# Attention P times V in plain 32-bit on the two column halves of the array, with P transposed and copied once

## The chip, the cores and the metric

The kernel runs on one core of a Trainium2 chip. A core has a matrix engine (PE, whose weight loads appear as PEld), three engines for elementwise work (DVE, ACT, POOL), and SP, which issues the DMAs. PE multiplies a stationary operand (loaded as weights) with a moving one and writes to PSUM; DVE and ACT bring results from PSUM to SBUF. The metric is the time of one execution on the device in microseconds.

## The reference

One layer of a token mixer with a feed-forward part: 1024 latent tokens and 256 context tokens of width 1024, everything in 32-bit floats. Eight attention heads of 64 share two key/value heads; beside them runs a bidirectional chunkwise mLSTM with four heads. What the change touches is the second product of the attention:

```python
p_loc = jnp.exp(s_loc - m)
p_ctx = jnp.exp(s_ctx - m)
inv = 1.0 / (p_loc.sum(-1, keepdims=True) + p_ctx.sum(-1, keepdims=True) + jnp.exp(sk - m))
o = (jnp.einsum('bnhgqk,bnkhd->bnqhgd', (p_loc * inv).astype(v.dtype), vw)
     + jnp.einsum('bnhgqc,bchd->bnqhgd', (p_ctx * inv).astype(v.dtype), vc))
...
mix_x = jnp.concatenate([att_x, ml_x], axis=-1) @ w_out[layer]
```

A query block of 128 tokens sees its own and the two neighbouring blocks of keys (one neighbour at the ends) and all context keys: three (or two) plus two key tiles of 128.

## The kernel before

The kernel has three stages: input projections and mLSTM state (to about 293 us of the profile), attention with the mLSTM output beside it (to about 480 us, the output projection begins in it), and the feed-forward part.

Large products run on operands of type `fp32r`, rounded below full 32-bit precision; each such matmul leaves one record in the trace. Where full precision is wanted, an operand is split: `split` (L62) lets ACT round it into a high part (L64) and DVE subtract that from the raw value for a low part (L65), and the product is built from two or three fp32r matmuls. A matmul on plain 32-bit operands needs no split.

The attention goes through 16 items, `items` (L714): row block `n` (eight of them), head group `g` (two). Loop pass `i` (L1052) does two things: the scores and softmax of item `i + 2` (class `Soft`: matmuls L972 and L973, masking on DVE L974, exponentials on ACT L983, normalisation on POOL L988), and the values of item `i` (class `Values`). The values come tile by tile of 128 keys, `nt` = 4 or 5 tiles an item, 76 in all:

- `tr(t)`: four transposes on PE (L1002) bring the tile of P for the four heads into a PSUM bank `pt` (three such banks, shared with the mLSTM values and the transposes of the mLSTM output), and `split` makes `th` on ACT and `tl` on DVE.
- `mm(t)`: two matmuls (L1012 with `th`, L1013 with `tl`) add to the bank `po`. Their stationary operand is `av2`, which holds V of the group's 64 columns twice, as high part and low part: 128 columns. So 64 rows of `po` hold the product with the high part of V, the other 64 that with the low part.
- `out()`: ACT copies one half of `po` (L1020), DVE adds the other (L1021) and writes the group's 64 rows of `mix`.

`av2` is made in the first stage by a split at L399. Beside that, passes 0 to 7 do the mLSTM output of a row block: scores (L862, DVE L867), values (L876, L880, then DVE L885 to L894 and ACT L892, L901), transposes back (L910, DVE L911). Passes 1 to 9 prepare slabs of the output weight: a load (L926) into the single buffer `wor`, a cast on ACT (L938), a subtraction on POOL (L939). The end of the loop and the last items carry the output projection (`omm`, rows `op`, L76 to L78).

The strings `PLAN_ML`, `PLAN` and `PLAN13` (L35 to L37) name the steps of a pass in the order in which they are handed over: T transposes, A scores, N softmax, M P times V, O its output, V mLSTM values, z, s, x other mLSTM steps, p the slab. From that a scheduler settles each engine's own order; an engine then works strictly through its own queue. What follows the loop stands in an order written out by hand (L1094 on).

Of the kernel before, what the change touches and what calls it, by code (L numbers as in the profile page):

```python
# [9 lines left out]
F32 = mybir.dt.float32  # L10
F32R = mybir.dt.float32r
# [3 lines left out]
ADD, SUB, MUL, MAX, MIN = ALU.add, ALU.subtract, ALU.mult, ALU.max, ALU.min  # L15

P = 128
# [3 lines left out]
NT = S // P  # L21
L = 256
NC_ = L // P
# [8 lines left out]
VSIL, VCONV, VGML, VBADA, VGPM, VGPF = 0, 16, 28, 32, 64, 72  # L32
VID = 80
NVEC = VID + P
PLAN_ML = "T0 A0 A1 A2 A3 T1 T2 T3 M0 M1 T4 V0 N0 M2 M3 M4 O z V1 w s N1 x p l"  # L35
PLAN = "T0 A0 A1 A2 A3 T1 T2 T3 N0 M0 T4 M1 M2 N1 M3 M4 O z p l"
PLAN13 = "T0 A0 A1 A2 A3 m T1 T2 P0 T3 N0 M0 T4 M1 P1 M2 N1 M3 P2 M4 O P3 l"  # L37
# [6 lines left out]
def body(tc, x, ctx, vecs, bcv, bada, gqm, gqf, wada, ws1, ws2, wt, wout, wfi, wfo,  # L44
         const, cosc, sinc, out):
    nc = tc.nc
    pe, act, dve, pool = nc.tensor, nc.scalar, nc.vector, nc.gpsimd
    dma = nc.sync.dma_start

    def open_pool(name, bufs=1, side="left", space=None):  # L50
        kw = dict(name=name, bufs=bufs, reuse_waits="tile")
        if space is not None:
            kw["space"] = space
        else:
            kw["side"] = side
        p = tc.tile_pool(**kw)
        return p, p.__enter__()
# [4 lines left out]
    def split(hi, lo, raw):  # L62

        act.copy(hi, raw)  # L64
        dve.tensor_tensor(lo, raw, hi.bitcast(F32), SUB)  # L65
# [77 lines left out]
    av2 = vp[1].tile([P, NT + NC_, 4, 64], F32R, name="av2")  # L143
    G = vp[1].tile([P, 4, 16, 4], F32, name="G")
    pool.memset(V[:, :, :, 128:129], 1.0)
    pool.memset(G, 0.0)
# [6 lines left out]
    hl = [htp[1].tile([P, 4, S], F32R, name=f"hl{i}") for i in range(2)]  # L153
# [48 lines left out]
    pts = {}  # L202
# [94 lines left out]
    for sec in (1, 0):  # L297
        pr = [pa.tile([4, 512], F32, name=f"pr{sec}{i}", tag="mm", bufs=4) for i in range(2)]
        for kt in range(KT):
            w = R(8 + kt, f"wa{sec}_{kt}", (D,))  # L300
# [16 lines left out]
            for n, (k, a, b) in enumerate(ops):  # L317
                if late and n < 2:
                    prep_t(1, True, (n,))
                for i in range(2):  # L320
                    r = pe.matmul(pr[i], a[:, k, :], b[:, i * 512:(i + 1) * 512], start=kt == 0 and n == 0,
                                  stop=kt == KT - 1 and n == len(ops) - 1)
# [19 lines left out]
        r = act.copy(r4[:, 0:512], pr[0])  # L342
# [7 lines left out]
        for q in range(2):  # L350
            t = (hcol, scol)[sec][:, q]
# [36 lines left out]
    def vrow(i):  # L388
        return V[:, i] if i < NT else Vc[:, i - NT]

    def s1(i):
        ps = slab(i, 272, w1h, w1l)
        sf = i + 2 if i < NT else i - NT
        sb = 9 - i if i < NT else 1 - (i - NT)
        dve.tensor_tensor(G[:, 0:2, sf, :], ps[:, 0:8].rearrange("p (k h) -> p k h", h=4),
                          bcr[:, 0:8].rearrange("p (k h) -> p k h", h=4), ADD)
        dve.tensor_tensor(G[:, 2:4, sb, :], ps[:, 8:16].rearrange("p (k h) -> p k h", h=4),
                          bcr[:, 8:16].rearrange("p (k h) -> p k h", h=4), ADD)
        split(av2[:, i, 0::3], av2[:, i, 1:3], ps[:, 16:144].rearrange("p (g v) -> p g v", v=64))  # L399
        act.copy(vrow(i)[:, 0, 0:128], ps[:, 144:272])  # L400

    NI = NT + NC_
# [19 lines left out]
    for i in range(NI):  # L422
# [7 lines left out]
        if i == 0:  # L430
            r = st[:, 13:14]
# [7 lines left out]
        if i in (1, 2):  # L439
            b = i - 1  # L440
# [138 lines left out]
    def T(i, name):  # L579
        return q2.tile([P, S], F32, name=name, tag=f"s{i}")  # L580
# [134 lines left out]
    NIT = len(items)  # L715
# [24 lines left out]
    for j, name in enumerate(TILES):  # L740
# [4 lines left out]
        ps = tproj(j, name in ("mk0", "mk1", "ak"))  # L745
        i = int(name[-1]) if name[-1].isdigit() else 0
# [4 lines left out]
        elif name == "ak":  # L751
# [14 lines left out]
        elif name.startswith("aq"):  # L766
            t = T(0, f"aq{i}")
# [6 lines left out]
        else:  # L774
            t = R(14 if i == 3 else 15, "so", (S,))
# [45 lines left out]
    for x_ in "hl":  # L821
        qa.tile([P, 4, P], F32R, name=f"t{x_}_", tag=f"pt{x_}", bufs=3)
# [4 lines left out]
    def bank():  # L827
        return pb.tile([P, 4, P], F32, name="pt", tag="pt", bufs=3)
# [161 lines left out]
    class Values:  # L990
        def __init__(self, i):
            self.n, self.g = items[i]
            self.pr = prs.pop(i)
            self.kb0, _, self.nb = blocks(self.n)
            self.nt = self.nb + 2
            self.po = pb.tile([P, 4, P], F32, name="po", tag="po", bufs=1)
            self.p = {}

        def tr(self, t):
            pt = bank()  # L1000
            for h in range(4):
                pe.transpose(pt[:, h, :], self.pr[:, h, 1 + t * P:1 + (t + 1) * P], ident)  # L1002
# [5 lines left out]
        def mm(self, t):  # L1008
            vt = self.kb0 + t if t < self.nb else NT + t - self.nb
            v2 = av2[:, vt, 2 * self.g:2 * self.g + 2].rearrange("p a v -> p (a v)")  # L1010
            th, tl = self.p.pop(t)
            pe.matmul(self.po, v2, th, start=t == 0, stop=False)  # L1012
            pe.matmul(self.po, v2, tl, start=False, stop=t == self.nt - 1)  # L1013

        def out(self):

            g = self.g
            rg, ot = slice(g * 64, g * 64 + 64), slice(64 - g * 64, P - g * 64)
            o2 = qa.tile([P, 4, P], F32, name="o2", tag="o2", bufs=1)
            act.copy(o2[rg], self.po[ot])  # L1020
# [20 lines left out]
    def omm(n, hf, ks):  # L1041

        h, l = mhl[n, hf]
        first, last = (0, 7) if n == 0 else (4, 3)
        for k in ks:
            j = 4 * hf + k
            for i in range(2):
                sl = slice(i * 512, (i + 1) * 512)
                mm3(ops_[n][:, sl], (h[:, k], l[:, k]), (wo[j][0][:, sl], wo[j][1][:, sl]), j == first, j == last)


    for i in range(NIT):  # L1052
        a = Soft(i + 2) if i + 2 < NIT else None
        b = Values(i)
        if i + 3 < NIT:
            q_load(i + 3)
        if i == NIT - 2:
            break
        wout_raw(i)
        for k in (PLAN_ML if i < NT else PLAN13 if i == NIT - 3 else PLAN).split():  # L1060
            op, n = k[0], int(k[1:] or 0)
            if op == "w" and i + 1 < NT:
                ml_load(i + 1)
            elif op == "T" and n < b.nt:
                b.tr(n)
            elif op == "M" and n < b.nt:
                b.mm(n)
            elif op == "O":
                b.out()
# [23 lines left out]

    order = tc.manual_schedule()  # L1094
    order.__enter__()
    def mm_t(b, *ts):
        for t in ts:
            b.mm(t)

    msplit(0, 1)  # L1100
    b.tr(0)
    b.tr(1)
    b.tr(2)
    omm(0, 1, range(1))
    mm_t(b, 0, 1)
    b.tr(3)
    omm(0, 1, range(1, 2))
    mm_t(b, 2, 3)
    b2 = Values(NIT - 1)
    b2.tr(0)  # L1110
    b.out()
    b2.tr(1)
    omm(0, 1, range(2, 3))
    b2.tr(2)
# [8 lines left out]
    b2.out()  # L1123
    order.__exit__(None, None, None)
    close(atp)
    close(aqp)
# [165 lines left out]
    th = {}  # L1292
# [73 lines left out]
    N1 = NT - 1  # L1366
# [359 lines left out]
    for p in range(4, HT):  # L1726
# [266 lines left out]
```

## Time and profile before

| | us |
|---|---|
| median of 3 runs | 1188.93 |
| lowest to highest | 1188.78 to 1191.32 |
| the profiled execution | 1189.32 |
| its span, first to last instruction | 1187.5 |
| granted PE clock over the span | 0.998 |
| PE busy in the span | 1164.6 |

A row of the profile's groups gives the line, the engine, the operation, what it writes and reads, shapes, count, then busy time, mean duration of one in ns, and the idle time before it with what ended it. A row of the timeline gives start and length in us. A count behind a row (x4) means neighbours that were joined. A matmul on plain 32-bit operands leaves two records, each with its weight load.

### The profile page before, as it was taken

To read this page: it belongs to the slowest core of one execution; us is meant where nothing else is said; L and a number is where in the kernel's file an instruction comes from. 1 tells how busy PE (TensorE), PEld (TensorE's weight loads), DVE (VectorE), ACT (ScalarE), POOL (GpSimd) and SP (SyncE) were. 2 spreads that over 40 slices of the span, in tenths; PEclk is the share of its full clock that TensorE was granted. 3 is DMA by queue.
4 is the path that set the end of the run, shared out by engine and by line. 5 is a ranking of instruction groups with operands and counts; after the bars stand their busy time and mean duration, and the time that the engine had idled before them with its cause. 6 is when DMAs were issued, how large, how long until landed. Compare 5 with 4: busy or idle time off the path is not lost.

```text
span 1187.5 us, 16397 instructions
## 1 busy us (share of the span) xinstructions
PE 1164.6 (98%) x5881; PEld 964.5 (81%) x5881; DVE 818.3 (69%) x1437; ACT 578.1 (49%) x1075; POOL 152.8 (13%) x204
## 2 busy tenths in 40 slices
PE   9899999999999989999999999999999999999997
PEld 3799888877888877888788888888888888888886
DVE  5864768863989984468767767776777656544566
ACT  6743442222877885777533334333333335434543
POOL 1550001225544550000000000000000000000000
PEclk9999999999999999999999999999999999999999
DMA  9522955648886713321242675656553557665853
GB/s 367 196 72 64 376 191 168 186 132 245 207 223 162 220 38 99 150 91 52 87 142 97 218 241 200 216 202 221 204 182 123 191 186 269 201 220 181 310 186 124
DMA packets 101992, 214.89 MB, mean 181 GB/s; under 512 B 10004, under 2 KB 39316, under 8 KB 100504
## 3 DMA queue, kind: packets, MB, share of 16 engines
q1 hardware_dynamic: 101912, 213.85, 54.4%
q8 instruction: 46, 0.75, 0.3%
q14 instruction: 34, 0.28, 0.1%
HBM read 157.19 MB, written 55.97 MB: 179 GB/s over the span
## 4 chain that ended last, share of the span: by engine, by line
PE 82%; DVE 10%; DMA 3%; ACT 2%; issue 2%; POOL 1%; SPq 0%; DVEq 0%; ACTq 0%; POOLq 0%
PE xv L78 8%; PE xv L76 8%; PE xv L77 8%; PE pt L78 6%; PE pt L76 6%; PE pt L77 6%; PE t L596 3%; PE t L595 2%; PE t L598 2%; PE op L78 2%; PE op L76 2%; PE op L77 2%; PE fx L76 2%; PE fx L78 2%; PE fx L77 2%
## 5 line engine op out<-in xcount | busy, mean ns | idle before, releaser
L65 DVE TENSOR_TENSOR fo<-fr,fo 128x1024 fp32r<-128x1024 f32 x77 | 92.7, 1222 | 70.9 <-ACT fo L64 70.6
L64 ACT CAST fo<-fr 128x1024 fp32r<-128x1024 f32 x77 | 79.7, 1052 | 73.9 <-PE pt L78 33.2
L595 PE MATMUL t<-hh,th 128*128 128x512 f32 x208 | 82.4, 396 | 0.0
L596 PE MATMUL t<-hl,th 128*128 128x512 f32 x208 | 81.7, 393 | 0.0
L1399 ACT CAST wS<-wr 128x512 fp32r<-128x512 f32 x88 | 54.2, 623 | 55.2 <-PE pt L78 36.6
L1401 DVE TENSOR_TENSOR wS<-wr,wS 128x512 fp32r<-128x512 f32 x88 | 60.4, 688 | 19.8 <-ACT wS L1399 19.7
L76 PE MATMUL xv<-tT,wS 128*128 128x512 f32 x168 | 65.6, 391 | 0.0
L78 PE MATMUL xv<-tT,wS 128*128 128x512 f32 x168 | 65.6, 391 | 0.0
L598 PE MATMUL t<-hh,tl 128*128 128x512 f32 x208 | 65.6, 393 | 0.0
L77 PE MATMUL xv<-tT,wS 128*128 128x512 f32 x168 | 65.5, 390 | 0.0
L76 PE MATMUL op<-woh,mh 128*128 128x512 f32 x128 | 51.0, 398 | 0.0
L77 PE MATMUL op<-wol,mh 128*128 128x512 f32 x128 | 50.0, 391 | 0.0
L78 PE MATMUL op<-woh,ml 128*128 128x512 f32 x128 | 50.0, 390 | 0.0
L1147 DVE TENSOR_TENSOR wr<-wr 128x512 f32<-128x512 f32 x66 | 45.5, 690 | 1.4
L1433 ACT ACTIVATE es<-es 128x512 f32<-128x512 f32 x22 | 13.9, 632 | 66.5 <-DVE es L1150 66.5
L595 PEld LDWEIGHTS t<-hh,th 128*128 128x128 f32 x208 | 39.1, 188 | 8.3 <-issue 0.3
L596 PEld LDWEIGHTS t<-hl,th 128*128 128x128 f32 x208 | 39.1, 188 | 7.8 <-issue 0.8
L598 PEld LDWEIGHTS t<-hh,tl 128*128 128x128 f32 x208 | 37.4, 188 | 6.9 <-issue 0.5
L76 PE MATMUL pt<-fo 128*128 128x512 f32 x110 | 42.8, 389 | 0.0
L77 PE MATMUL pt<-fo 128*128 128x512 f32 x110 | 42.8, 389 | 0.0
L78 PE MATMUL pt<-fo 128*128 128x512 f32 x110 | 42.8, 389 | 0.0
L972 PE MATMUL s<-k,qh 128*128 128x256 f32 (+1 forms) x128 | 40.5, 327 | 0.9 <-DVE sm L974 0.8
(1016 smaller groups left out, 3403.1 us busy)
## 6 DMA issues: line engine op xcount, KB each, us to landing
wr<-in_wfi SPq DMA_DIRECT2D x44, 512.0 KB, 4.8
wb<-in_wada SPq DMA_DIRECT2D x24, 512.0 KB, 5.8
s_d<-a SPq DMA_DIRECT2D x22, 512.0 KB, 6.8
bt<-in_wfo SPq DMA_DIRECT2D x44, 256.0 KB, 4.0
tb_d<-bt SPq DMA_DIRECT2D x11, 1024.0 KB, 3.9
fr<-s_d SPq DMA_DIRECT2D x44, 256.0 KB, 4.4
fr<-tb_d SPq DMA_DIRECT2D x44, 256.0 KB, 4.3
fr<-a_d SPq DMA_DIRECT2D x33, 256.0 KB, 4.5
```

Of the source, the lines that this page charges most:

```text
L64: act.copy(hi, raw)
L65: dve.tensor_tensor(lo, raw, hi.bitcast(F32), SUB)
L76: pe.matmul(ps, a[0], b[0], start=first, stop=False, **kw)
L77: pe.matmul(ps, a[0], b[1], start=False, stop=False, **kw)
L78: pe.matmul(ps, a[1], b[0], start=False, stop=last, **kw)
L595: pe.matmul(o, wh[:, kt], m[0], start=f, stop=False)
L596: pe.matmul(o, wh[:, kt], m[1], start=False, stop=False)
L598: pe.matmul(o, wl[:, kt], m[0], start=False, stop=l)
L972: pe.matmul(o, qh[:, h, :], k2[g][:, kc], start=True, stop=False)
L1147: dve.tensor_tensor(out, a, b, SUB)
L1399: act.copy(w[:, 0], raw)
L1401: dve.tensor_tensor(w[:, 1], raw, w[:, 0].bitcast(F32), SUB)
```

## The change

P is no longer split. `tr` copies the transposed tile once, ACT the even tiles and DVE the odd ones, into one of nine buffers `ts`. V is kept in plain 32-bit, 64 columns per group (`av`, half the size of `av2`), with one ACT copy in place of its split. P times V is one plain matmul per tile and group with 64 stationary columns: group 0 writes rows 0 to 63 of `po`, group 1 rows 64 to 127, and for each tile the two follow one another. It is done for both groups of a row block together, in the odd passes: `M0` does tiles 2, 1, 0, `M1` tiles 4, 3. One ACT copy takes the whole bank to `mix`. The step strings are new, with one for even and one for odd passes, and so is the order behind the loop.

```diff
-PLAN_ML = "T0 A0 A1 A2 A3 T1 T2 T3 M0 M1 T4 V0 N0 M2 M3 M4 O z V1 w s N1 x p l"
-PLAN = "T0 A0 A1 A2 A3 T1 T2 T3 N0 M0 T4 M1 M2 N1 M3 M4 O z p l"
+PLAN_ML = ("T0 A0 A1 A2 A3 T1 T2 T3 V0 N0 T4 z V1 w s N1 x p l", "T0 A0 A1 A2 A3 T1 T2 V0 N0 T3 M0 T4 z V1 w s M1 O N1 x p l")
+PLAN = ("T0 A0 A1 A2 A3 T1 T2 T3 N0 T4 N1 z p l", "T0 A0 A1 A2 A3 T1 T2 T3 N0 M0 T4 N1 M1 O z p l")
+NTS = 9
...
-        split(av2[:, i, 0::3], av2[:, i, 1:3], ps[:, 16:144].rearrange("p (g v) -> p g v", v=64))
+        act.copy(av[:, i], ps[:, 16:144].rearrange("p (g v) -> p g v", v=64))
...
-            th = qa.tile([P, 4, P], F32R, name="th_", tag="pth", bufs=3)
-            tl = qa.tile([P, 4, P], F32R, name="tl_", tag="ptl", bufs=3)
-            split(th, tl, pt)
-            self.p[t] = th, tl
+            self.p[t] = ts = qa.tile([P, 4, P], F32, name="ts_", tag="pts", bufs=NTS)
+            if t % 2:
+                dve.tensor_copy(ts, pt)
+            else:
+                act.copy(ts, pt)
...
-            pe.matmul(self.po, v2, th, start=t == 0, stop=False)
-            pe.matmul(self.po, v2, tl, start=False, stop=t == self.nt - 1)
...
-            act.copy(o2[rg], self.po[ot])
-            dve.tensor_tensor(mix[self.n][rg, 0:4, :], self.po[rg], o2[rg], ADD)
...
+        for t in ts:
+            vt = a.kb0 + t if t < a.nb else NT + t - a.nb
+            for g, x_ in ((1, b), (0, a)):
+                r = pe.matmul(pos[a.n][64 * g:64 * g + 64], av[:, vt, g], x_.p.pop(t), start=first and t == ts[0],
+                              stop=not more and t == ts[-1])
...
+    def pv_out(n):
+        act.copy(mix[n][:, 0:4, :], pos.pop(n))
...
-    mm_t(b2, 0, 1)
-    b2.tr(3)
+    pv(b, b2, range(4), False, False)
     omm(0, 1, range(3, 4))
-    mm_t(b2, 2, 3)
```

Two places show how the engines' queues change. The first is PE in pass 7, the second of the two passes of row block 3, from the transposes of its tiles on (`pr` is the pass's P, `th` and `tl` the split parts, `ts` the copies, `cs`, `qz`, `V`, `wl` the mLSTM values' operands). Before:

```order
L1002 MATMUL pt<-vec,pr__3728 128x128 x8
L1012 MATMUL po<-th__4111,av_91 128x512
L1002 MATMUL pt<-vec,pr__3728 128x128 x8
L1013 MATMUL po<-tl__4112,av_91 128x512
L1012 MATMUL po<-th__4144,av_91 128x512
L1013 MATMUL po<-tl__4145,av_91 128x512
L1002 MATMUL pt<-vec,pr__3728 128x128 x4
L1012 MATMUL po<-th__4153,av_91 128x512
L876 MATMUL pt<-cs_2558,qz_2970 128x129 x2
L880 MATMUL pt<-V,wl_4056 128x129 x2
L1013 MATMUL po<-tl__4154,av_91 128x512
L1012 MATMUL po<-th__4162,av_91 128x512
```

and now, in the same pass:

```order
L1001 MATMUL pt<-vec,pr__3627 128x128 x8
L876 MATMUL pt<-cs_2548,qz_2939 128x129 x2
L880 MATMUL pt<-V,wl_3919 128x129 x2
L1001 MATMUL pt<-vec,pr__3627 128x128 x4
L1019 MATMUL po<-ts__4011,av 64x512
L1019 MATMUL po<-ts__3852,av 64x512
L1019 MATMUL po<-ts__4004,av 64x512
L1019 MATMUL po<-ts__3845,av 64x512
L1019 MATMUL po<-ts__3973,av 64x512
L1019 MATMUL po<-ts__3814,av 64x512
L1001 MATMUL pt<-vec,pr__3627 128x128 x4
```

The P times V matmuls no longer stand singly between other work, but in a block of six, two for each tile, with the copies of passes 7 and 6 in turn; pass 6 has none.

The second is ACT about passes 8 and 9, around the casts of two slabs of the output weight (L938; L983 are the exponentials). Before:

```order
L938 CAST woh_4256<-wor_4104 128x1024
L983 ACTIVATE pr__4382,sm<-pr__4382,sm 128x641 x3
L64 CAST th__4399<-pt 128x512
L1020 COPY o_4361<-po 64x512
L64 CAST th__4432<-pt 128x512
L983 ACTIVATE pr__4382,sm<-pr__4382,sm 128x641
L64 CAST th__4441<-pt 128x512
L938 CAST woh_4370<-wor_4270 128x1024
L64 CAST th__4450<-pt 128x512
```

and now:

```order
L938 CAST woh_4107<-wor_3966 128x1024
L983 ACTIVATE pr__4111,sm<-pr__4111,sm 128x641
L1006 COPY ts__4165<-pt 128x512
L1006 COPY ts__4184<-pt 128x512
L1006 COPY ts__4225<-pt 128x512
L983 ACTIVATE pr__4209,sm<-pr__4209,sm 128x641 x3
L1006 COPY ts__4263<-pt 128x512
L938 CAST woh_4197<-wor_4120 128x1024
```

Copies of the even tiles take the place of the casts of all tiles, the copy of the output (L1020) is gone from the even pass, and a tile's copy still stands in the queue between the slab casts.

More of the change, by code (lines that the diff above doesn't have):

```diff
@@ L34 @@
 NVEC = VID + P
-PLAN_ML = "T0 A0 A1 A2 A3 T1 T2 T3 M0 M1 T4 V0 N0 M2 M3 M4 O z V1 w s N1 x p l"
-PLAN = "T0 A0 A1 A2 A3 T1 T2 T3 N0 M0 T4 M1 M2 N1 M3 M4 O z p l"
-PLAN13 = "T0 A0 A1 A2 A3 m T1 T2 P0 T3 N0 M0 T4 M1 P1 M2 N1 M3 P2 M4 O P3 l"
+PLAN_ML = ("T0 A0 A1 A2 A3 T1 T2 T3 V0 N0 T4 z V1 w s N1 x p l", "T0 A0 A1 A2 A3 T1 T2 V0 N0 T3 M0 T4 z V1 w s M1 O N1 x p l")
+PLAN = ("T0 A0 A1 A2 A3 T1 T2 T3 N0 T4 N1 z p l", "T0 A0 A1 A2 A3 T1 T2 T3 N0 M0 T4 N1 M1 O z p l")
+PLAN13 = "T0 A0 A1 A2 A3 m T1 T2 P0 T3 N0 M0 T4 P1 N1 P2 M1 O P3 l"
+NTS = 9
 WR = ((1, 2), (4, 5), (6, 7), (0, 3), (14, 15), (10, 13), (12, 8), (9, 11))
@@ L142, in body @@
     vp[1].tile([P, 88], F32, name="padv")
-    av2 = vp[1].tile([P, NT + NC_, 4, 64], F32R, name="av2")
+    av = vp[1].tile([P, NT + NC_, 2, 64], F32, name="av")
     G = vp[1].tile([P, 4, 16, 4], F32, name="G")
@@ L820, in body @@
     qa = atp[1]
-    for x_ in "hl":
-        qa.tile([P, 4, P], F32R, name=f"t{x_}_", tag=f"pt{x_}", bufs=3)
+    qa.tile([P, 4, P], F32, name="ts_", tag="pts", bufs=NTS)
     qa.tile([P, 80], F32, name="padq")
@@ L995, in __init__ @@
             self.nt = self.nb + 2
-            self.po = pb.tile([P, 4, P], F32, name="po", tag="po", bufs=1)
             self.p = {}
@@ L1002, in tr, with pv @@
                 pe.transpose(pt[:, h, :], self.pr[:, h, 1 + t * P:1 + (t + 1) * P], ident)
-            th = qa.tile([P, 4, P], F32R, name="th_", tag="pth", bufs=3)
-            tl = qa.tile([P, 4, P], F32R, name="tl_", tag="ptl", bufs=3)
-            split(th, tl, pt)
-            self.p[t] = th, tl
[L1008 to L1011, printed above, removed]
-            pe.matmul(self.po, v2, th, start=t == 0, stop=False)
[L1013 to L1020, printed above, removed]
-            dve.tensor_tensor(mix[self.n][rg, 0:4, :], self.po[rg], o2[rg], ADD)
+            self.p[t] = ts = qa.tile([P, 4, P], F32, name="ts_", tag="pts", bufs=NTS)
[3 more added lines that the diff above has]
+                act.copy(ts, pt)
+    pos = {}
+    def pv(a, b, ts, more, pin=True):
+        ts = [t for t in ts if t < a.nt][::-1]
+        first = a.n not in pos
+        if first:
+            pos[a.n] = pb.tile([P, 4, P], F32, name="po", tag="po", bufs=1)
+        for t in ts:
[3 more added lines that the diff above has]
+                              stop=not more and t == ts[-1])
+                if pin and (t != ts[0] or not g):
+                    tc.keep_in_program_order(r)
+    def pv_out(n):
+        act.copy(mix[n][:, 0:4, :], pos.pop(n))
     tc.keep_in_program_order(act.preload_act_table_set("natural_log_exp_and_others"))
@@ L1049, in omm @@
                 mm3(ops_[n][:, sl], (h[:, k], l[:, k]), (wo[j][0][:, sl], wo[j][1][:, sl]), j == first, j == last)
+    b = None
     for i in range(NIT):
         a = Soft(i + 2) if i + 2 < NIT else None
-        b = Values(i)
+        b0, b = b, Values(i)
         if i + 3 < NIT:
@@ L1059, in body @@
         wout_raw(i)
-        for k in (PLAN_ML if i < NT else PLAN13 if i == NIT - 3 else PLAN).split():
+        for k in (PLAN_ML[i % 2] if i < NT else PLAN13 if i == NIT - 3 else PLAN[i % 2]).split():
             op, n = k[0], int(k[1:] or 0)
@@ L1065, in body @@
                 b.tr(n)
[L1066 to L1069, printed above, removed]
+            elif op == "M" and i % 2:
+                pv(b0, b, ((0, 1, 2), (3, 4))[n], not n)
+            elif op == "O" and i % 2:
+                pv_out(b.n)
             elif op == "A" and a:
@@ L1095, in body @@
     order.__enter__()
-    def mm_t(b, *ts):
-        for t in ts:
-            b.mm(t)
     msplit(0, 1)
@@ L1104, in body @@
     omm(0, 1, range(1))
-    mm_t(b, 0, 1)
     b.tr(3)
-    omm(0, 1, range(1, 2))
-    mm_t(b, 2, 3)
     b2 = Values(NIT - 1)
     b2.tr(0)
-    b.out()
+    omm(0, 1, range(1, 2))
     b2.tr(1)
+    b2.tr(2)
     omm(0, 1, range(2, 3))
-    b2.tr(2)
+    b2.tr(3)
     msplit(1, 1)
     act.preload_act_table_set("sqrt_and_others")
-    mm_t(b2, 0, 1)
-    b2.tr(3)
+    pv(b, b2, range(4), False, False)
     omm(0, 1, range(3, 4))
-    mm_t(b2, 2, 3)
     ops_[1] = pb.tile([P, 1024], F32, name="op", tag="s", bufs=2)
     omm(1, 1, range(4))
-    b2.out()
+    pv_out(b.n)
     order.__exit__(None, None, None)
```

## The prediction

> **What bounds the kernel now.** I read the page's totals first, then the busy time by stage, then single stretches of the timeline. The totals:
>
> ```profile
> span 1187.5 us, 16397 instructions
> PE 1164.6 (98%) x5881; PEld 964.5 (81%) x5881; DVE 818.3 (69%) x1437; ACT 578.1 (49%) x1075; POOL 152.8 (13%) x204
> ```
>
> PE looks full, but a PE row lasts from its start to the end of its result, so rows overlap and a late start hides in the busy time. The change touches four stretches; for each: length, busy time (and count) of PE, weight loads, DVE, ACT, POOL, then granted clock, DMA share and GB/s.
>
> ```profile
> 299.00:410.80 111.80, 108.64 (x780) 96.17 (x780) 101.66 (x307) 91.61 (x257) 55.75 (x65) 1.00 0.78 202
> 410.80:444.70 33.90, 28.92 (x188) 24.66 (x187) 29.62 (x68) 28.64 (x62) 18.13 (x22) 1.00 0.27 73
> 444.70:480.00 35.30, 35.01 (x176) 28.37 (x175) 16.36 (x26) 18.58 (x34) 2.73 (x4) 1.00 0.40 140
> 480.00:1187.50 707.50, 701.41 (x3114) 578.71 (x3112) 472.22 (x656) 317.13 (x514) 0.96 (x1) 1.00 0.52 177
> ```
>
> The first row is the attention with the mLSTM work beside it (eight items and part of a ninth), the second attention alone (four items), the third its end with the output projection, the fourth the feed-forward part, which the change does not touch. In the first, DVE is busy 101.7 of 111.8 us (91%). I take one steady pair of items, a row block with its two head groups:
>
> ```profile
> 361.70:387.00 25.30, 24.93 (x182) 21.85 (x181) 22.92 (x71) 19.81 (x57) 10.91 (x14) 1.00 0.60 139
> ```
>
> How much of these 25.3 us does PE need? I take its pace from starts of neighbouring rows where nothing is late:
>
> ```profile
> 345.68 0.61 PE L876 MATMUL pt<-cs,qz 128*128 128x129 f32 x4
> 346.12 0.61 PE L880 MATMUL pt<-V,wl 128*128 128x129 f32 x4
> ...
> 347.04 0.34 PE L972 MATMUL s<-k,qh 128*128 128x384 f32 x1
> ...
> 347.62 0.34 PE L972 MATMUL s<-k,qh 128*128 128x384 f32 x1
> ...
> 349.88 0.71 PE L862 MATMUL s<-mq,mk 64*128 64x128 f32 x8
> ...
> 350.53 0.71 PE L876 MATMUL pt<-cs,qz 128*128 128x129 f32 x4
> ...
> 352.11 0.60 PE L1002 MATMUL pt<-vec,pr__3179 128*128 128x128 f32 x4
> ```
>
> ```profile
> L1002 PE MATMUL pt<-vec,pr__4596 128*128 128x128 f32 x20 | 3.2, 272 | 0.0
> ```
>
> Four mLSTM value records take 0.44 us, the scores of one head 0.58, the mLSTM scores 0.65. Four transposes last 0.60, a single one 0.272, so one follows another after (0.60 - 0.27) / 3 = 0.11. The fp32r matmul 128x512, and one in plain 32-bit, which leaves two records in the trace for each matmul written:
>
> ```profile
> 15.51 0.63 PE L321 MATMUL pr<-hh,cs 128*4 128x512 f32 x2
> 15.97 0.63 PE L321 MATMUL pr<-hl,cs 128*4 128x512 f32 x2
> ```
>
> ```profile
> 6.03 1.88 PE L321 MATMUL pr<-wa,cz 128*4 128x512 f32 x4
> ```
>
> ```profile
> L321 PE MATMUL pr<-wa,cz 128*4 128x512 f32 x24 | 11.3, 592 | 0.3 <-DMA wa<-in_wada 0.3
> ```
>
> Two fp32r matmuls take 15.97 - 15.51 = 0.46 us, so one takes 0.23. A plain record takes (1.88 - 0.59) / 3 = 0.43, a plain matmul 0.86. One item of five tiles thus needs 4 x 0.58 scores + 20 x 0.11 transposes + 10 x 0.23 P times V + 8 x 0.44 values + 0.65 + 0.44 (four more transposes) = 11.4 us, a pair 22.8. So PE loses **2.5 of 25.3 us to waiting**. What for shows in such places:
>
> ```profile
> 355.38 0.69 DVE L65 TENSOR_TENSOR tl__3600<-pt,th__3599 128x512 fp32r<-128x512 f32 x1 [0.58 <-ACT th__3599 L64]
> ...
> 356.13 0.19 PEld L1013 LDWEIGHTS po<-tl__3600,av 128*128 128x128 f32 x1 [0.54 <-DVE tl__3600 L65]
> ```
>
> ACT rounds a tile, then DVE subtracts, then PE may go on: the split is in the chain twice, and it is DVE's largest single load here.
>
> **The change, part by part.** *P is copied once.* Per tile an ACT copy and a DVE subtraction become one copy, on ACT for even tiles and DVE for odd ones. DVE's subtractions (L65) in the two attention stretches, and after them the additions (L1021) that merged the two halves of an output:
>
> ```profile
> 299.00:410.80 111.80, 29.26 (x44) 1.00 0.78 202
> 410.80:444.70 33.90, 15.30 (x23) 1.00 0.27 73
> ```
>
> ```profile
> 299.00:410.80 111.80, 5.48 (x8) 1.00 0.78 202
> 410.80:444.70 33.90, 2.76 (x4) 1.00 0.27 73
> ```
>
> What takes their place, by its nearest rows:
>
> ```profile
> L346 DVE COPY Vc<-pr 4x512 f32<-4x512 f32 x2 | 1.4, 675 | 0.1
> ```
>
> ```profile
> L1020 ACT COPY o<-po 64x512 f32<-64x512 f32 x16 | 9.3, 581 | 2.4 <-PE po L1013 2.1
> ```
>
> A DVE copy of 512 elements from PSUM takes 0.675, no less than the subtraction (29.26 / 44 = 0.67); an ACT copy 0.58. Per pair DVE loses ten subtractions and two additions and gains four copies: -10 x 0.67 - 2 x 0.69 + 4 x 0.675 = -5.4 us, from 22.9 to 17.5. ACT loses ten casts and two copies and gains six copies and one: -5 x 0.58 = -2.9, from 19.8 to 16.9. Neither can be the bound after that. The copies have nine buffers; the pair's tenth tile needs one that the P times V block ahead of it on PE has read, so this adds no wait.
>
> *P times V.* Per tile and pair of groups, four fp32r matmuls (0.92 us) become two plain ones of 64 columns. Alone these would take 2 x 0.86 = 1.72; side by side 0.86. The one place in this trace where matmuls of 64 columns alternate between the column halves, in plain 32-bit, is the state update, with its neighbours and its single duration:
>
> ```profile
> 206.41 0.39 PE L598 MATMUL t<-hh,tl 128*128 128x512 f32 x1
> 206.72 1.10 PE L704 MATMUL pu<-V,mkc 128*64 128x129 f32 x16
> 207.76 0.50 PE L598 MATMUL t<-hh,tl 128*128 128x512 f32 x1
> ```
>
> ```profile
> L704 PEld LDWEIGHTS pu<-V,mkc x112: 132/136/137, 206.7 to 286.1; 128*64 128x64 f32 x112
> L704 PE MATMUL pu<-V,mkc x112: 271/273/325, 206.7 to 286.2; 128*64 128x129 f32 x112
> ```
>
> Sixteen records take 1.10 - 0.27 = 0.83 us, 0.055 each, where the full-width L876 of the same 129 elements took 0.11 each: two run at once. The way in costs 206.72 - 206.41 - 0.23 = 0.08, the way out (207.76 against 207.55 + 0.11) 0.10. I take 0.86 per tile pair, and 0.18 per block, two to three blocks per pair of items: 5 x 0.86 + 2.5 x 0.18 = 4.75 against 20 x 0.23 = 4.60, so **+0.15 us per pair**. The bounds are 4.3 (no cost of changing) and 8.6 plus blocks (no overlap at 512 columns).
>
> On the hiding of weight loads the Trainium skill speaks against this: "TensorE: Matmul & The Clock Gate", Part 3, The mechanism, has a load overlap a running matmul only where the row groups differ, and the two halves share all rows. By that rule the loads would stand in the open. By that the sum would end at 1202 (below) instead of 1181. The trace disagrees: 16 loads of 0.136 are 2.2 us, and the whole block took 1.10.
>
> *What is late next.* PE's need per pair is 22.8 + 0.15 = 23.0, so at most 2.3 us of 25.3 go. P times V now sits in the odd item alone: without it PE needs 9.1 us in the even item, against DVE's 17.5 / 2 = 8.8 and ACT's 8.4, so there the three still hand work to one another nearly in step, and I leave 1.0 us of waiting per pair. Gain 1.3 to 1.4 per pair; the first stretch holds 111.8 / 25.3 = 4.4 pairs: **6 us** (bounds 0 and 10). DMA, busy 0.78 of that stretch, then comes to 0.82, and stays hidden.
>
> *Attention alone, 410.8 to 444.7.* Four items need 4 x (2.32 + 2.2 + 2.3) = 27.3 of 33.9 us. Most of the rest lies where ACT stands at the cast of a w_out slab, with the casts of P queued behind it:
>
> ```profile
> 407.63 2.40 POOL L939 TENSOR_TENSOR wol<-wor,woh 128x1024 fp32r<-128x1024 f32 x1
> ...
> 410.17 0.55 SPq L926 DMA_DIRECT2D wor<-in_wout  x1
> ...
> 415.56 1.04 ACT L938 CAST woh<-wor 128x1024 fp32r<-128x1024 f32 x1 [2.27 <-DMA wor<-in_wout]
> ...
> 416.68 2.40 POOL L939 TENSOR_TENSOR wol<-wor,woh 128x1024 fp32r<-128x1024 f32 x1 [1.87 <-ACT woh L938]
> ...
> 420.07 0.54 SPq L926 DMA_DIRECT2D wor<-in_wout  x1
> ...
> 424.78 1.04 ACT L938 CAST woh<-wor 128x1024 fp32r<-128x1024 f32 x1 [1.58 <-DMA wor<-in_wout]
> ```
>
> The slab has one buffer: POOL's subtraction ends (410.03), the load goes out, lands 5.4 us later, ACT 1.04, POOL 2.40, then the next. That ring is 9 us long whatever DVE does, and two items of 6.8 us of PE work run inside it in 20 us. I take **2 us** (bounds 0 and 3.5).
>
> *The rest.* In the first stage V's own split goes:
>
> ```profile
> L65 DVE TENSOR_TENSOR av<-slab,av 128x128 fp32r<-128x128 f32 x10 | 2.9, 285 | 2.4 <-ACT av L64 2.3
> ```
>
> That is 2.9 us of DVE beside a PE that is busy throughout; I take a tenth of it: 0.3. At the end PE had 35.01 of 35.3; there the last P times V starts with the tile transposed last and waits for its copy, 0.27 + 0.68, which takes the place of a wait for the last split: 0, bounds -1 and +1.
>
> The profiled execution took 1189.32 us, 0.4 above the median of 1188.93. Sum: 1189.3 - 6 - 2 - 0.3 = **1181 us**.
>
> **Rivals.** *Nearly all waiting goes:* 10 + 3.5 + 0.3 + 1 = 15 us, 1174. For it: DVE and ACT fall to some 70% of a pair; against it: the even item. *Hand-overs stay:* the three PSUM banks for transposes and mLSTM values, and the in-order queues, keep PE waiting as now although DVE idles; then about 2 to 3 us, 1187. For it: PE's wait now comes in pieces of half a microsecond behind single instructions. *Slower: the halves do not overlap at 512 columns.* Then a pair's P times V takes 8.6 + 0.45 instead of 4.6 us, 4.45 more. The first stretch needs 111.8 - 4.4 x 2.5 + 4.4 x 4.45 = 120.4, with some waiting 121 (+9); the second 27.3 + 8.9 = 36.2, with some waiting 37 (+3); the end, without slack and with some six and a half tile pairs, +6: 1207. It decides from the point where a quarter of the second matmul is left in the open (76 tiles / 2 x 0.86 = 33 us, of which 8.3 are the forecast's gain). Against it stands the L704 block; for it, that the block streamed 129 columns and not 512.
>
> *Weight loads in the open:* 152 records that each first wait 0.136 for their load are 21 us of PE work on top of the forecast, 1202. No row speaks for it, and L704 against it. It is what the Trainium skill's rule above would give.
>
> **How the numbers follow.** The forecast's own range, 1177 to 1185, gets 0.55; nearly all 0.13; hand-overs 0.20; no overlap 0.08; open loads 0.02; something not listed 0.02. The range runs from 1173 to 1188 and leaves the slower cases out. A measurement tells some 0.2%, 2.4 us: a third of the hand-over case lies within it. Faster 0.81, same 0.08, slower 0.11.
>
> **What would show it.** Right: plain 64-column rows in pairs a few ns apart, a block of six in about 2.6 us; DVE busy under 80 us where it was 101.7, PE's rows closer, a pair in 24 us; the w_out ring still 9 us. Wrong: 0.43 between single P times V rows; PE waiting for a bank with DVE idle; the feed-forward part longer than 707.5 us.

## The result and the profile after

| | before | after |
|---|---|---|
| median, us (4 runs each, side by side) | 1190.12 | 1181.13 |
| lowest to highest | 1188.78 to 1191.89 | 1181.01 to 1181.93 |
| ratio of the times, with its 95% interval | | 0.9926 [0.9913, 0.9938] |
| the profiled execution | 1189.32 | 1181.93 |

The change saves 0.74%, as much as was forecast. Its parts are another matter. The totals of the changed kernel's page:

```profile
span 1180.2 us, 16216 instructions
PE 1161.6 (98%) x5881; PEld 948.0 (80%) x5881; DVE 781.8 (66%) x1367; ACT 558.0 (47%) x1035; POOL 154.0 (13%) x204
```

In both kernels PE has 5881 records, a tile and group leaving two each time (before: one each with `th` and `tl`; now: the two records of a plain matmul). So a point in the work can be found by counting records: windows that begin at 0 and hold equally many PE records end at nearly the same PE work. That is a safer ruler here than a single event, since the change moves P times V past any of them; but records of different kinds differ in price, so which kinds have been done has to be counted too. Columns: length, then busy time (and count) of PE, weight loads, DVE, ACT, POOL, then granted clock, DMA share and GB/s. Before:

```profile
0.00:410.80 410.80, 399.30 (x2408) 332.74 (x2409) 300.06 (x690) 213.74 (x468) 130.97 (x177) 1.00 0.64 200
0.00:444.70 444.70, 428.22 (x2594) 357.40 (x2595) 329.68 (x756) 242.37 (x529) 149.10 (x199) 1.00 0.61 190
0.00:480.00 480.00, 463.23 (x2768) 385.77 (x2769) 346.04 (x782) 260.96 (x562) 151.83 (x203) 1.00 0.59 186
```

After:

```profile
0.00:300.10 300.10, 291.58 (x1630) 237.45 (x1631) 198.69 (x373) 122.14 (x211) 76.75 (x113) 0.99 0.59 198
0.00:408.40 408.40, 396.73 (x2408) 324.05 (x2409) 281.28 (x647) 202.87 (x445) 132.31 (x177) 1.00 0.64 201
0.00:436.04 436.04, 424.37 (x2594) 343.77 (x2596) 301.06 (x697) 226.49 (x496) 150.72 (x200) 1.00 0.62 194
0.00:472.40 472.40, 459.94 (x2768) 369.13 (x2769) 309.44 (x712) 240.25 (x522) 153.05 (x203) 1.00 0.60 190
```

At the 2408th record the changed kernel is 2.4 us ahead, at the 2594th 8.7, at the 2768th 7.6. At the last point the kinds done are the same in both. At the 2408th the changed kernel has done 10 P times V records fewer (76 against 86), one of the scores fewer and 11 transposes more; at the 2594th 5 P times V records and 3 of the output projection fewer and 8 transposes more. At 0.22 us for a record of P times V (0.43 a pair), 0.17 for the scores, 0.23 for the projection and 0.11 for a transpose, it still owes 1.1 and 0.9 us of work there, so at equal work it is some 1.3, 7.8 and 7.6 us ahead. The long stretch with the mLSTM work brought little, and the short one of attention alone 6.3 us by the count and 6.5 at equal work, the reverse of the forecast. A pair of items shows the same (182 PE records, first before, then after):

```profile
361.70:387.05 25.35, 24.98 (x182) 21.90 (x181) 22.97 (x71) 19.83 (x58) 10.96 (x14) 1.00 0.60 139
```

```profile
360.80:385.96 25.16, 24.39 (x182) 19.55 (x181) 18.32 (x63) 17.21 (x53) 11.04 (x13) 1.00 0.51 134
```

DVE has 4.65 us less to do, ACT 2.6, and the pair is 0.2 us shorter, where 1.3 to 1.4 was forecast. P times V itself looks as described, in a timeline of PE:

```profile
366.15 0.61 PE L880 MATMUL pt<-V,wl 128*128 128x129 f32 x4
366.69 0.64 PE L1019 MATMUL po<-ts__3681,av 128*64 128x512 f32 x1
366.70 0.64 PE L1019 MATMUL po<-ts__3526,av 128*64 128x512 f32 x1
367.17 0.59 PE L1019 MATMUL po<-ts__3681,av 128*64 128x512 f32 x1
367.18 0.59 PE L1019 MATMUL po<-ts__3526,av 128*64 128x512 f32 x1
367.70 0.66 PE L1001 MATMUL pt<-vec,pr__3299 128*128 128x128 f32 x4
```

The two groups' records start 10 ns apart: the halves overlap at 512 columns. The four L880 records are through at 366.15 + 0.44 = 366.59, the transposes start at 367.70: a block of one tile pair takes 1.11 us, 0.25 more than its 0.86.

In the second stretch, the slab loads, in timelines of SP and of ACT:

```profile
405.82 0.34 SPq L926 DMA_DIRECT2D wor<-in_wout  x1
...
412.89 0.34 SPq L926 DMA_DIRECT2D wor<-in_wout  x1
```

```profile
409.36 1.05 ACT L938 CAST woh<-wor 128x1024 fp32r<-128x1024 f32 x1 [0.38 <-DMA wor<-in_wout]
417.09 1.05 ACT L938 CAST woh<-wor 128x1024 fp32r<-128x1024 f32 x1
```

The ring is 412.89 - 405.82 = 7.1 us long, not 9 to 10, and ACT's waits of 2.27 and 1.58 us there are down to 0.38 and none. What PE waited for in that stretch, before (us in total, times, longest):

```profile
PE po L1012 <- ACT th__4450 L64: 2.1, 1, 2.1
PE po L1012 <- ACT th__4560 L64: 1.5, 1, 1.5
PE pt L1002 <- DVE tl__4645 L65: 0.6, 1, 0.6
PE pt L1002 <- DVE tl__4747 L65: 0.3, 1, 0.3
PE po L1012 <- DVE mix L1021: 0.3, 1, 0.3
```

That is 4.8 us; after, the same view of 408.4 to 436 has no row. SP's queue shows why the slabs came sooner. Before, three loads of queries stood ahead of one slab and two ahead of the next:

```profile
408.15 1.24 SPq L724 DMA_DIRECT2D qh<-aq_dh  x2
409.49 0.57 SPq L724 DMA_DIRECT2D ql<-aq_dl  x1
410.17 0.55 SPq L926 DMA_DIRECT2D wor<-in_wout  x1
```

In the changed kernel the scheduler puts both slabs ahead of these queries. The forecast had not read SP's order.

### The profile page after: what moved, and what is told of

Its sections match the earlier page's. It is cut to its first block, busy times and chain, and to the rows that moved or that the text cites. A ratio compares the mean times of both kernels' runs of the same rounds, so it can differ in the third digit from the quotient of the medians.

```text
span 1180.2 us, 16216 instructions
## 1 busy us (share of the span) xinstructions
PE 1161.6 (98%) x5881; PEld 948.0 (80%) x5881; DVE 781.8 (66%) x1367; ACT 558.0 (47%) x1035; POOL 154.0 (13%) x204
## 4 chain that ended last, share of the span: by engine, by line
PE 89%; DMA 4%; DVE 4%; ACT 1%; issue 1%; SPq 0%; POOL 0%; DVEq 0%; ACTq 0%
PE xv L79 8%; PE xv L77 8%; PE xv L78 8%; PE pt L77 6%; PE pt L78 6%; PE pt L79 6%; PE po L1019 3%; PE t L597 3%; PE t L596 3%; PE t L599 3%; PE pt L1001 3%; PE op L77 3%; PE op L79 2%; PE op L78 2%; PE fx L77 2%; PE slab L77 2%
```

## The experiments

Times are medians, ratios against the kernel before on the same chip. "At record n" is the time of that PE record in the profile, by windows like those above.

| run | us | ratio [95%] |
|---|---|---|
| halves in turn | 1190.07 | 0.9998 [0.9989, 1.0007] |
| one-tile blocks | 1188.39 | 0.9986 [0.9977, 0.9995] |
| free casts on DVE | 1198.70 | 1.0074 [1.0061, 1.0087] |
| additions on DVE | 1207.84 | 1.0145 [1.0131, 1.0158] |
| all copies on DVE | 1190.51 | 1.0000 [0.9991, 1.0009] |
| before, one copy | 1191.98 | 1.0009 [1.0000, 1.0019] |
| before, one copy in items 2 to 13 | 1182.13 | 0.9935 [0.9922, 0.9948] |
| the same and slab first | 1182.78 | 0.9937 [0.9924, 0.9950] |
| before, slab first | 1186.13 | 0.9959 [0.9946, 0.9971] |
| slab twice | 1182.67 | 0.9931 [0.9919, 0.9943] |
| last block later | 1180.69 | 0.9921 [0.9907, 0.9934] |
| whole blocks, last block later | 1180.25 | 0.9921 [0.9905, 0.9937] |

**Do the halves need to alternate in the queue?**

```diff
-        for t in ts:
-            for g, x_ in ((1, b), (0, a)):
+        for g, x_ in ((1, b), (0, a)):
+            for t in ts:
```

> Same work as the changed kernel (1181.1 us), but within a block of P times V all matmuls of one column half stand first in the queue, then all of the other; before, the halves alternated tile by tile. Theory A, only neighbours in the queue overlap: a block of k tile pairs then takes 4k-1 record times of 0.43 us instead of 2k; with 7 blocks of three pairs (2.15 us more each), 6 of two (1.29) and one of four (3.0) that is 25.8 us more work, 1200 to 1207 us. Theory B, each half works through a queue of its own that holds a whole block: records still in pairs a few ns apart, 1180 to 1182 us. In between, if only part of a block is looked ahead at.

Neither: 1190.07 us, 8.9 more than the changed kernel. The queue holds 4011, 4004, 3973 of group 1, then 3852, 3845, 3814 of group 0; PE's timeline:

```profile
395.11 1.07 PE L1019 MATMUL po<-ts__4011,av 128*64 128x512 f32 x2
396.02 0.59 PE L1019 MATMUL po<-ts__4004,av 128*64 128x512 f32 x1
396.03 0.64 PE L1019 MATMUL po<-ts__3852,av 128*64 128x512 f32 x1
...
396.88 0.59 PE L1019 MATMUL po<-ts__3973,av 128*64 128x512 f32 x1
396.94 0.59 PE L1019 MATMUL po<-ts__3845,av 128*64 128x512 f32 x1
...
397.80 1.02 PE L1019 MATMUL po<-ts__3814,av 128*64 128x512 f32 x2
```

The first matmul runs alone, then the fourth of the queue starts 10 ns behind the second and ahead of the third, and the last runs alone: four slots of 0.86 instead of three. Blocks of two tile pairs lost nothing. So PE starts a matmul of the free half past one that still waits for its own half, but no further; a lone slot in each of seven blocks (6.0 us), two in the last block of four (1.7) and one more in the first row block are 8.6 of the 8.9 us. It also prices the rival of halves that do not overlap: every slot that ran alone was paid in full.

**What does a block cost?** In one run the blocks are single tile pairs, each as soon as it can be (`M0` to `M4` spread over the pass):

```diff
-                pv(b0, b, ((0, 1, 2), (3, 4))[n], not n)
+                pv(b0, b, (n,), n < b.nt - 1)
```

> The changed kernel with P times V in blocks of one tile pair instead of three and two, each as soon as the tile of the odd item is copied: 12 to 14 more blocks on the way up to 437 us, as some blocks still meet in the queue. Price theory (a block costs 0.2 to 0.25 us beside its records, the way in and out between fp32 rows of the full array and column halves): 2.5 to 3.5 us more, 1183.5 to 1184.5 us. Cover theory (small blocks fall into places where PE waits for a bank): 1180 to 1182 us.

```profile
0.00:410.45 410.45, 400.83 (x2408) 323.67 (x2409) 282.64 (x648) 203.79 (x448) 133.25 (x178) 1.00 0.64 200
```

Up to there it has 19 blocks instead of 11 and is 410.45 - 408.40 = 2.05 us behind the changed kernel, which would be 0.256 a block. But it had reached record 1630, ahead of any block, 1.2 us sooner (298.9 against 300.1), and at record 2408 it has done four P times V records more and four transposes fewer, 0.4 us of work. From the same start and at equal work it is some 2.8 us longer, 0.35 a block, waits included. So blocks cost time, as the price theory has it, but this run alone does not fix the price. The other 5 us (by the medians) came later: seven more blocks, and a slab that came late again:

```profile
415.45 1.05 ACT L938 CAST woh<-wor 128x1024 fp32r<-128x1024 f32 x1 [5.13 <-DMA wor<-in_wout]
```

**What is the single copy worth alone?** The kernel before, with one copy and no other part of the change:

```diff
-            split(th, tl, pt)
-            self.p[t] = th, tl
+            if t % 2:
+                dve.tensor_copy(th, pt)
+            else:
+                act.copy(th, pt)
+            self.p[t] = th, th
```

> The kernel before the change with P rounded once by one copy (ACT even tiles, DVE odd) and its low part left out: both matmuls of a tile use the high part, so PE has the same work in the same places, but the subtraction on DVE and the second hand-over are gone. If the split in the chain is what cost the mLSTM stretch its 2 us: that stretch gains 2 or more, at equal PE work, and the whole comes to 1181 to 1186 us. If the pairs, blocks and new order brought it: 1187 to 1190 us.

The high part goes into both matmuls of a tile, so the result is about twice what it should be, and the run serves for the time alone. It came out at 1191.98 us, which says little, for in its profile PE lost 3.2 us in one wait at the start, where DVE's first maskings came late, and 4.4 in another behind the loop, where DVE stood before a late load of another tensor; and the granted clock was 0.50 for 3.4 us at 297.1 and again at 471.2:

```profile
PE s L971 <- DVE sm L973: 3.2, 1, 3.2
...
PE op L78 <- DVE ml L65: 4.4, 1, 4.4
```

Between record 1630 (302.3) and 2408 (408.6), clear of both places, it took 106.3 us, where the kernel before took 111.75. So the same with the single copy only in items 2 to 13:

```diff
+            one = 2 <= self.i < 14
-            split(th, tl, pt)
-            self.p[t] = th, tl
+            split(th, tl, pt) if not one else dve.tensor_copy(th, pt) if t % 2 else act.copy(th, pt)
+            self.p[t] = th, th if one else tl
```

> As the run with one copy in the kernel before (low part of P left out, both matmuls of a tile use the high part), but only for items 2 to 13, so that the engines' orders at the start and in the part behind the loop, where that run lost 3.7 and 6 us to other things, stay those of before. In SP's queue the last but one slab stands ahead of the queries of item 14, the last one behind those of item 15. If the split's hand-over and DVE's load are the larger cause: at equal PE work some 4 to 5 us less up to 425 us, the whole 1183 to 1187 us. If pairs and blocks are: within 1.5 us of before there.

```profile
0.00:405.55 405.55, 396.56 (x2408) 334.10 (x2409) 289.18 (x668) 209.34 (x454) 131.85 (x179) 1.00 0.64 202
0.00:436.30 436.30, 424.28 (x2594) 358.80 (x2595) 312.14 (x724) 234.11 (x508) 150.22 (x201) 1.00 0.62 194
```

```profile
359.95:383.54 23.59, 23.59 (x182) 21.76 (x181) 19.63 (x65) 18.58 (x54) 11.64 (x14) 1.00 0.65 161
```

1182.13 us, as fast as the whole change. It is 5.25 us ahead at record 2408, with the same work done but for one transpose and one score, where the changed kernel is 2.4 ahead by the count and 1.3 at equal work. ACT waits for no slab up to there in either kernel, so this much comes with the copy. The pair takes 23.59 us: 1.76 less than before and 1.57 less than with the changed P times V. What it wins after that record is not the copy's alone, since the last slab but one is issued ahead of the queries here too. And it drops P's low part and takes the high part twice. What the plain 32-bit product buys is that one copy holds all of P, and the column halves keep that product nearly as cheap as the split one.

**Load or hand-over?** All copies on DVE:

```diff
-            if t % 2:
-                dve.tensor_copy(ts, pt)
-            else:
-                act.copy(ts, pt)
+            dve.tensor_copy(ts, pt)
```

> The changed kernel with all copies of transposed tiles on DVE, none on ACT: DVE gets 40 more copies of 0.68 us, some 27 us over the attention, and goes to about 96 to 98 of 106 us in the first stretch; ACT loses as many of 0.58 us. Load theory: most of the gain in that stretch is lost, 1184 to 1187 us. Chain theory: a tile's chain is as long as before (0.68 instead of 0.58 for six of ten) and PE's remaining waits in the first stretch were for copies on ACT, so 1179.5 to 1182 us.

```profile
0.00:411.60 411.60, 398.36 (x2408) 324.18 (x2409) 292.83 (x671) 189.96 (x418) 132.66 (x178) 1.00 0.63 200
```

The whole gain is gone (1190.51). The chain theory as I had put it falls: a tile is still copied once, yet the kernel is 3.2 us later at record 2408 and loses most of the rest after it. But load by itself is not the answer either: up to that record DVE is busy 292.83 us here and 289.18 in the run with one copy in items 2 to 13, which is 6 us faster there. One difference is that there every second tile leaves its bank by the other engine; P times V differs too, and PE's order is not that of the changed kernel (15 blocks instead of 18), so this is not isolated. Two attempts to load DVE with work off the chain measured something else. The casts,

```diff
+            if t < 4:
+                dj = qa.tile([P, 4, P], mybir.dt.bfloat16, name="dj", tag="dj", bufs=1)
+                dve.tensor_copy(dj, mask[:, 0:4])
```

> The changed kernel with one more DVE instruction for each of the first four tiles of an item: a cast of 512 columns of the mask into a scratch tile that nobody reads, 64 in all, so that DVE has about as much to do as before the change, while no chain is longer. Load theory (the gain came because DVE was 91% busy): DVE in the first attention stretch goes from 78.6 us to about 95, and most of the 5.6 us won there come back, 1184 to 1187 us. Chain theory (the gain came because the split stood twice in the way between a transpose and its product): the stretch stays within 1.5 us of 106.2, 1181 to 1182.5 us.

were free to run early, and did (windows of that line alone: length, DVE busy and count):

```profile
300.00:363.70 63.70, 29.54 (x49) 0.94 0.66 180
363.70:480.00 116.30, 3.67 (x9) 1.00 0.49 144
```

so 49 of 64 stood in the first third, where DVE was busy 62.89 of 63.7 us and the kernel lost 15 us, and in the rest there was neither load nor loss. Not all of the 15 need be waiting: the granted clock was 0.94 there, which takes up to (1 - 0.94) x 63.7 = 3.8 us of PE's time. The additions, one for each of the first four tiles (`dve.tensor_tensor(dj, ts, mask[:, 0:4], ADD)`),

> The changed kernel with one more DVE instruction for each of the first four tiles of an item, an addition that reads the tile's copy and writes a scratch tile that nobody reads, 64 in all. Unlike the free casts of the run before, which went ahead in the queue, each must stay behind its copy, so DVE's load is spread as before the change (about 0.67 us each, 22.9 us per pair of items). Load theory: 1184 to 1188 us, PE waiting for DVE's masking and copies. Chain theory: 1181 to 1182.5 us.

stayed in place, but took 62.59 us in all instead of the planned 43, since some waited for POOL:

```profile
364.11 2.36 POOL L939 TENSOR_TENSOR woxl<-wor,woxh 128x1024 fp32r<-128x1024 f32 x1
364.49 2.53 DVE L1005 TENSOR_TENSOR dj<-ts__3536,mask 128x512 bf16<-128x512 f32 x1
```

Neither prices the load of before the change. In both PE paid for DVE work ahead of the maskings and copies (26.7 us for these 62.59), up to some 6 us of it by the granted clock, 0.97 over the 200 us from 290 to 490.

**The slab.** The kernel before, with only SP's queue changed:

```diff
+        with tc.issue_after(wlast[i - 3]) if i in (11, 12) else ExitStack():
+            if i + 3 < NIT:
+                q_load(i + 3)
```

> The kernel before the change (1190.1 us), with one edit: in SP's queue the loads of the queries of items 14 and 15 stand behind the loads of the last two slabs of the output weight, as the changed kernel has them, where before three and two of these query loads stood ahead. The queues of all other engines are the same, word for word. Queue theory (the changed kernel won 6.4 of its 8.6 us between 409 and 433 us because these two slabs were issued ahead of the queries, landed in 3.5 instead of 5.3 us, and ACT no longer stood at their casts with the copies of P behind it): 1184 to 1187 us, and ACT's two waits of 2.27 and 1.58 us shrink to under 1. Copy theory (won because half of the copies are on DVE and there are nine buffers): 1189 to 1190.5 us.

```profile
0.00:442.50 442.50, 427.95 (x2594) 358.13 (x2595) 329.96 (x757) 242.08 (x529) 148.75 (x199) 1.00 0.61 191
```

```profile
PE po L1012 <- ACT th__4450 L64: 1.1, 1, 1.1
```

1186.13 us, so 4.4 us (3.5 to 6.4 by the interval) from the order of five small loads; in the one profile it is 2.2 at record 2594, and PE's wait of 2.1 is 1.1, that of 1.5 is gone. The opposite, in the changed kernel, with both slabs loaded twice:

```diff
-                dma(wraw[j], wout[j])
+                [dma(wraw[j], wout[j]) for _ in range(1 + (i in (8, 9)))]
```

> The changed kernel (1181.1 us) with each of the last two slabs of the output weight loaded twice into the same buffer, the second load behind the first, so that ACT gets them some 3 us later; PE's order is the same up to about 418 us. Queue theory: ACT stands at the two casts again with copies of P behind it, PE loses 3 to 6 us there, 1184 to 1187 us. Copy theory: the copies on DVE and the buffers carry PE over it, 1181 to 1182.5 us.

```profile
414.31 1.05 ACT L938 CAST woh<-wor 128x1024 fp32r<-128x1024 f32 x1 [2.56 <-DMA wor<-in_wout]
426.99 1.04 ACT L938 CAST woh<-wor 128x1024 fp32r<-128x1024 f32 x1 [3.86 <-DMA wor<-in_wout]
```

```profile
PE po L1019 <- ACT ts__4467 L1006: 1.4, 1, 1.4
PE pt L1001 <- POOL pr__4479 L988: 0.5, 1, 0.5
```

ACT waits longer than it did before the change, and the waits that PE's view names are 1.9 us instead of 4.8; the kernel gives back 1.5 by the medians (1182.67), less than the intervals tell apart. In its profile, the slowest of its five executions (1183.88), it loses more: from record 2408 to 2594 it takes 31.0 us, 0.4 of it more work, against 27.6 in the changed kernel and 33.9 before. So a slab that comes later than before costs the changed kernel some 3 of the 6.5 us won in that stretch, and it keeps the rest: both theories held a part. Copy and slab order together, in the kernel before:

> The same with one more edit: in SP's queue the last slab too stands ahead of the queries of item 15, as in the changed kernel. So it has the single copy and the slab order of the changed kernel, but neither its column halves, nor its pairs and blocks, nor nine buffers. If copy and slab order make up the whole gain: 1181 to 1183 us. If the two overlap or the blocks carry a part of it: 1183.5 to 1186 us.

1182.78 us, not to be told from the run with the copy in items 2 to 13. The last slab was issued ahead of the queries and still came late (ACT waited 2.95 us for it; with the queries ahead 1.93), and so did the last but one, which stands ahead of its queries in both runs (3.03 against 1.18). In this profile the granted clock was also 0.50 for 3.4 us from 417.2 on, 1.7 us of PE's time. So the place in SP's queue is not all that sets when a slab lands; what else does stays open, and whether copy and slab order add up does too.

**The end.** In the changed kernel PE waits once behind the loop:

```profile
454.10 0.64 PE L1019 MATMUL po<-ts__4746,av 128*64 128x512 f32 x1 [0.78 <-DVE ts__4746 L1004]
```

```diff
-    pv(b, b2, range(4), False, False)
     omm(0, 1, range(3, 4))
+    pv(b, b2, range(4), False, False)
```

> The changed kernel with one edit at the end: the last block of P times V stands behind the eighth quarter of the first output projection instead of ahead of it. In the changed kernel PE stood there some 1.0 to 1.4 us for the copy of the tile that was transposed last. If that wait was real: 1179.7 to 1180.3 us and no wait at that block. If the work it is moved past hides nothing because the next product waits instead: 1181 us.

The wait is gone; 1180.69 against 1181.13 us is within the two intervals. The last run adds whole blocks: the transposes of the fourth tile pinned ahead of the first block in the mLSTM passes.

> The changed kernel (1181.1 us) with two edits: in the mLSTM passes the first block of P times V is no longer cut in two by the transposes of the fourth tile, which now stand ahead of it (16 blocks in all instead of 18), and the last block stands behind the eighth quarter of the output projection, as in the run that tried this alone (1180.7 us). SP's order of slabs and queries is that of the changed kernel. Price theory (a block costs about 0.25 us beside its records): 1179.7 to 1180.4 us. Rival: ahead of an unbroken block PE waits for the third tile's copies, which the cut had covered: 1181 us or more.

1180.25 us, the lowest median here, at 0.9921 [0.9905, 0.9937], but not to be told from the run before it, nor by the interval from the changed kernel (0.9926). In the profile, with two blocks instead of three in a pair, two passes take 24.82 us (from the first mLSTM score matmul, L862, of one pass at 350.61 to that of the next but one at 375.43) instead of 25.15 in the changed kernel (352.39 to 377.54): 0.33 for one block, waits included.

## Why the forecast came out, step by step

**The total** of 1181 was right by luck: two terms missed in opposite directions and nearly cancelled.

*P is copied once* was sized right: 1.3 to 1.4 us a pair forecast, 1.76 in the run that has only this, 5.25 us up to record 2408 against the term's 6. In the changed kernel, though, that stretch gained only 1.3 at equal work (2.4 from record 1630 on, which came 1.1 us late; 3.1 in the profile of the run with the last block later, the same code up to there), for the next two reasons. DVE's 17.5 and ACT's 16.9 us a pair came out at 18.3 and 17.2.

*P times V, +0.15 us per pair* was too small. The records run as read from L704, 0.43 a pair. But a block costs 0.25, not 0.18, and the scheduler cuts a pair's five tiles into three blocks, not two and a half: 3 x 0.25 + 5 x 0.86 = 5.05 against 4.60, +0.45.

*I leave 1.0 us of waiting per pair* failed by more. With 22.8 + 0.45 of work in 25.16 us, 1.9 are left, where the run with the single copy and the old P times V leaves 23.59 - 22.8 = 0.8. The view of PE's waits names 0.8 of the 1.9, the row below; the rest are gaps too small for it, and some may be work that 22.8 leaves out. The even item without P times V was seen as the weak place, and there it stands: PE wants a bank whose tile ACT has not yet copied.

```profile
383.07 0.30 PE L910 MATMUL pt<-vec,hs 128*128 128x128 f32 x1 [0.77 <-ACT ts__3891 L1006]
```

Together, 0.45 and 1.1, these give back 1.57 of the 1.76 us; that is near the rival "hand-overs stay", true in this stretch. That the waiting comes from the move of P times V into the odd pass was read from this row and the pair, not tried alone.

*Attention alone, 2 us*, measured 6.3 (6.5 at equal work), beyond its bound of 3.5. The step that failed is "that ring is 9 us long whatever DVE does": its length held 5.4 us for a load that stood behind queries in SP's queue, an order which the change moved. The slab order alone gave 2.2 in the profile and 4.4 by the medians. The run with one copy in items 2 to 13, which has one of the two slabs ahead, gave (444.7 - 410.8) - (436.3 - 405.55) = 3.15; the run with the copy and both slabs ahead, whose slabs came late and whose clock fell, 33.9 - (439.1 - 405.4) = 0.2. So the slabs have a large share in the 6.5; how the rest divides stays open.

*The end, 0 (bounds -1 and +1)*: (472.40 - 436.04) - (480 - 444.7) = +1.06 by the count, of which 0.9 is the work that the changed kernel still owed at record 2594; at equal work it is +0.2, with the wait of 0.78 above in it, so this term held. *V's split, 0.3*: not to be seen. Record 1630 comes 1.1 us later (300.1 against 299.0), with the same kinds done in both; but the run with one-tile blocks and the last run, with the same first stage, have it at 298.9 and 299.4, so this much differs from one execution to the next.

*The slower rivals* fell as argued. The Trainium skill's page "TensorE: Matmul & The Clock Gate", Part 3, The mechanism, would have the loads of two halves with the same rows in the open; the records 0.43 us a pair leave no room for them.

## What to carry to other kernels

Check a forecast at equal work, not at an event that the change may move: by the last mLSTM row the first stretch seemed to have won its 6 us, by the count of PE records 2.4, and with the kinds of these records counted too it was 1.3. When code moves, read the DMA queue's order as closely as PE's: the place of five small loads, changed alone, was worth half as much as this whole change. And side-by-side column halves pay per block, so keep blocks whole; that the other passes need work enough to cover their copies is read from one wait and not tried.

## What the runs showed of the hardware

- PE does not keep matmuls of different column halves in program order: the fourth in the queue started at 396.03, the third at 396.88. The Trainium skill's "TensorE: Matmul & The Clock Gate", Part 3, The mechanism, has matmuls strictly first in, first out, without reordering; for plain 32-bit matmuls on column halves this trace shows otherwise, by one matmul.
- Going from full-array plain 32-bit rows to column halves and back costs 0.25 us a block (1.11 instead of 0.86; 0.33 by the pair with one block fewer, waits included). The Trainium skill's "TensorEngine Tiling (Array Packing)", Key Properties, says that a change of tiling mode drains the engine; here is its price.
- A DVE addition of two SBUF operands took 2.53 us beside a POOL subtraction of 2.36, 0.98 in the mean of 64 where 0.67 was planned. The Trainium skill's "SBUF — State Buffer", SBUF: two separate sides, has such a pair lock each other out; the trace agrees.
